# More modulation blocks summed by VectorE, in PSUM; weight splits in quarters, the later ones on GpSimd alone

## The chip, the cores and the metric

One core of a Trainium2 chip runs the whole kernel. The metric is the device time of one execution in microseconds (us), and the median of three such runs of the kernel before is 1456.18 us. The engines are named as the profile names them: PE is TensorE (matmuls), PEld its weight loads, DVE is VectorE, ACT is ScalarE, POOL is GpSimd, SP the engine that issues the loads. Every engine takes its instructions in order.

## What is computed

A layer of a transformer-like encoder on 256 positions of width 2048, all in float32. The parts that matter here, condensed from the reference:

```python
mod = c_act @ w_ada[l] + b_ada[l]
sh1, sc1, g1, sh2, sc2, g2 = [m[:, None, :] for m in jnp.split(mod, 6, axis=-1)]
h = rms_norm(x, g_mix[l]) * (1 + sc1) + sh1
z = h @ w_in                                  # 2048 -> 4616 columns
y = concat([gmlp(u, v), pool(p), attention(q, k, va, fz)]) @ w_out
x = x + g1 * y
h = rms_norm(x, g_ffn[l]) * (1 + sc2) + sh2
x = x + g2 * moe_ffn(h, ...)                  # 16 experts, the router picks 2 for each position
```

The modulation `mod` is one vector (`c_act`, 2048 values) times a matrix of 2048 by 12,288: much weight for little arithmetic. The projections `w_in` and `w_out` are dense products with 256 rows.

## The kernel before

**Split products.** A float32 product is made of three fast ones: each weight tile is split into a high part (a ScalarE cast, L174) and a remainder (one subtraction, L175, on VectorE or GpSimd), written into a buffer `whl`; `mm3` (L177) then issues three matmuls. A weight tile is [128, 4, 512], 1 MB. `halves` (L407) splits it in two halves of [128, 1024] with three buffers of 8 KB for each partition; the first half's remainder is VectorE's, the second half's the engine that `WSPLIT` (for each chunk) or `WSO` (output projection) names. A piece, two halves, has 24 matmuls of 128x512 and needs two PSUM banks `pm`.

**Chunks.** The input projection runs over five chunks of rows of `w_in` (`CHUNKS`, L53): two of 2 row blocks, three of 4. Chunks one and two use `small_piece` (L458), with tiles of two row blocks by 1024 columns: nine blocks of 512 columns, each of 12 matmuls. The others use `piece`, nine pieces each. The first chunk copies its sums into `z` with ScalarE (L436); the others add them with VectorE (L438). The last chunk is woven with the attention (`att_step`, L613, in four parts a to d, for eight heads), gMLP, and pooling. Four pooling bands (`band`, L366) are built in the first chunk by VectorE and GpSimd together. After the chunks comes the output projection (four column blocks of four tiles each), then routing and the experts.

**Modulation blocks.** The modulation's matrix comes in 24 blocks of up to 512 columns, each in steps of 1 MB (four products of 512 columns or eight of 256). A block is done by TensorE in a PSUM bank `accs` (`ada_parts`, L250; a step of four is eight matmul records), or by VectorE as a running sum in SBUF (`sum_parts`, L272, L290 and L292). The strings in L68 say which: `M1A` and `M1B` for shift and scale of the next chunk, `M2A` and `M2B` for the second half of the layer, `G1` for the gate ahead of the output projection. `M1` uses `accs[0]`, `M2` `accs[1]`.

**Order.** The program's order on each engine is written out by hand: `step` (L155) prepares a piece of work (load, split) at once and puts its run (matmuls or sums) into a queue `todo`, which holds up to `LOOK` split pieces and `LOOK_ALL` in all; `PLAN` and `LAST` say after which piece which modulation step comes (`n` and `m`), and when its results are used. Loads go through a ring of six 1 MB halves.

## Time and profile before

| | us |
|---|---|
| median of three runs | 1456.18 (1456.14 to 1457.46) |
| profiled execution | 1460.89 |
| its span in the trace | 1459.1 |
| chunk one, two | 32.37, 41.41 |
| chunk three, four | 67.17, 66.95 |
| last chunk, with attention | 136.99 |
| output projection and the start of the routing | 125.05 |

The lower rows are stretches of the profiled execution. From some 497 us on the routing and the experts run. A row of the timeline begins with its start and its length; in brackets stands the idle time ahead of it on that engine and what ended it. A window's row gives the busy time of PE, PEld, DVE, ACT and POOL in that stretch, then TensorE's granted clock as a share of 2.4 GHz, the DMA share and the rate.

### The profile page before, as it was taken

The numbers are of one execution on the slowest core, as the hardware profiler recorded it, in microseconds if no ns is written. First come the engines' busy times: TensorE is split into PE (matmuls) and PEld (weight loads), VectorE is DVE, ScalarE is ACT, GpSimd is POOL, SyncE is SP. The second block draws the span as 40 slices with busy tenths as digits, with TensorE's granted clock in tenths as the row PEclk, the third lists the DMA queues.
The fourth block names the chain that finished last, engine by engine and source line by source line (L and its number), as shares of the span: only waits on it lengthen the run. The fifth ranks groups of instructions, "written<-read, shape, count | busy, mean of one in ns | idle before, by whom it ended". The sixth has DMA issues, their size and how long they took to land.

```text
span 1459.1 us, 17581 instructions
## 1 busy us (share of the span) xinstructions
PE 1264.6 (87%) x6930; PEld 703.1 (48%) x6930; DVE 693.5 (48%) x1184; ACT 412.8 (28%) x720; POOL 146.0 (10%) x89
## 2 busy tenths in 40 slices
PE   5999999999989997999968999789997879858865
PEld 3666666666667563575324753337633222222221
DVE  3757483555798372795125961169711202202112
ACT  4433333646333240583003840028400000000000
POOL 0423332311333100000000000000000000000000
PEclk8999999999999998999999999999999999979988
DMA  9787787888877868998999989999899999999997
GB/s 378 270 348 281 281 340 265 303 351 328 349 278 270 310 288 367 427 428 317 421 426 427 426 318 419 424 428 426 333 408 428 427 426 427 428 426 428 426 426 303
DMA packets 49207, 539.14 MB, mean 369 GB/s; under 512 B 5464, under 2 KB 5592, under 8 KB 7008
## 3 DMA queue, kind: packets, MB, share of 16 engines
q1 hardware_dynamic: 47664, 534.79, 89.7%
q10 hardware_dynamic: 1456, 3.17, 0.6%
q8 instruction: 56, 0.92, 0.2%
q14 instruction: 31, 0.25, 0.0%
HBM read 535.85 MB, written 2.10 MB: 369 GB/s over the span
## 4 chain that ended last, share of the span: by engine, by line
PE 38%; DMA 27%; DVE 5%; issue 1%; ACT 1%; DVEq 0%; ACTq 0%
PE lbank L170 28%; DMA ring<-in_e_down_dram 11%; DMA ringl<-in_e_gu_dram 9%; DMA ring<-in_e_gu_dram 7%; PE bank L170 5%; PE pm L170 3%; DVE grow L292 2%; PE ada L170 1%; DVE whl L175 1%; DVE el L175 1%; ACT el L174 0%; DVE grow L290 0%; PE lgp L170 0%; DVE hid L1225 0%; PE pt L170 0%
## 5 line engine op out<-in xcount | busy, mean ns | idle before, releaser
L170 PE MATMUL pm<-whl,hT 128*128 128x512 f32 x1120 | 300.9, 405 | 19.9 <-DVE whl L175 10.8
L170 PEld LDWEIGHTS pm<-whl,hT 128*128 128x128 f32 x1120 | 212.3, 193 | 93.6 <-issue 15.3
L170 PE MATMUL lbank<-ringl,xr 128*32 128x256 f32 (+1 forms) x1152 | 143.7, 496 | 38.0 <-DMA ringl<-in_e_gu_dram 37.8
L170 PE MATMUL lbank<-el,xs 128*128 128x512 f32 x576 | 139.9, 401 | 10.2 <-ACT el L174 7.4
L170 PE MATMUL lbank<-ring,xr 128*32 128x256 f32 (+1 forms) x864 | 105.6, 491 | 34.1 <-DMA ring<-in_e_gu_dram 34.0
L174 ACT CAST whl<-ring 128x1024 fp32r<-128x1024 f32 x96 | 99.0, 1048 | 125.7 <-PE pm L170 70.7
L175 POOL TENSOR_TENSOR whl<-ring,whl 128x1024 fp32r<-128x1024 f32 x43 | 108.3, 2518 | 231.7 <-ACT whl L174 211.0
L170 PEld LDWEIGHTS lbank<-el,xs 128*128 128x128 f32 x576 | 109.3, 192 | 41.0 <-ACT el L174 10.6
L170 PE MATMUL bank<-y,gt 128*128 128x512 f32 x240 | 119.1, 619 | 0.0
L1284 DVE TENSOR_TENSOR xa<-xa,bank 128x512 f32<-128x512 f32 x120 | 82.5, 687 | 69.9 <-PE bank L170 69.9
L170 PEld LDWEIGHTS lbank<-ringl,xr 128*32 128x32 f32 (+1 forms) x1152 | 51.9, 128 | 129.8 <-issue 68.5
L170 PE MATMUL lbank<-ring,hidT 128*64 128x512 f32 (+1 forms) x576 | 103.8, 624 | 11.5 <-DMA ring<-in_e_down_dram 11.5
L1275 DVE TENSOR_TENSOR y<-lbank,g2w 128x512 f32<-128x512 f32 x60 | 41.5, 691 | 145.7 <-PE lbank L170 145.7
L174 ACT CAST el<-ring 128x512 fp32r<-128x512 f32 x144 | 89.7, 623 | 29.6 <-PE lbank L170 21.7
L175 DVE TENSOR_TENSOR el<-ring,el 128x512 fp32r<-128x512 f32 x144 | 92.7, 688 | 0.0
L175 DVE TENSOR_TENSOR whl<-ring,whl 128x1024 fp32r<-128x1024 f32 x53 | 72.2, 1368 | 35.9 <-ACT whl L174 33.6
L170 PE MATMUL ada<-ring,cact 128*1 128x512 f32 (+1 forms) x648 | 75.1, 566 | 15.6 <-DMA ring<-in_w_ada_dram 14.4
L1171 ACT COPY gt<-bank 128x256 f32<-128x256 f32 x15 | 5.6, 372 | 287.9 <-PE bank L1169 287.9
L170 PEld LDWEIGHTS lbank<-ring,xr 128*32 128x32 f32 (+1 forms) x864 | 39.5, 128 | 98.4 <-DMA ring<-in_e_gu_dram 48.4
L1225 DVE TENSOR_TENSOR hid<-hid,lbank 128x512 f32<-128x512 f32 x12 | 8.2, 687 | 165.0 <-PE lbank L170 164.7
L170 PE MATMUL lbank<-el,hidT 128*128 128x512 f32 x288 | 74.8, 411 | 12.2 <-DVE el L175 8.3
L438 DVE TENSOR_TENSOR z<-z,pm 128x512 f32<-128x512 f32 x72 | 49.0, 685 | 71.8 <-PE pm L170 71.8
(363 smaller groups left out, 1219.3 us busy)
## 6 DMA issues: line engine op xcount, KB each, us to landing
ringl<-in_e_gu_dram SPq DMA_DIRECT2D x60, 2048.0 KB, 20.1
ring<-in_w_ada_dram SPq DMA_DIRECT2D x90, 1024.0 KB, 7.0
ring<-in_e_gu_dram SPq DMA_DIRECT2D x45, 2048.0 KB, 24.4
ring<-in_e_down_dram SPq DMA_DIRECT2D x45, 2048.0 KB, 25.6
ring<-in_w_in_dram SPq DMA_DIRECT2D x35, 1024.0 KB, 7.0
ringm<-in_e_gu_dram SPq DMA_DIRECT2D x15, 2048.0 KB, 21.7
ringm<-in_e_down_dram SPq DMA_DIRECT2D x15, 2048.0 KB, 21.5
ring<-in_w_out_dram SPq DMA_DIRECT2D x12, 1024.0 KB, 8.3
```

The lines of the kernel that those rows point to most:

```text
L170: E.matmul(out, lhsT=lhsT, rhs=rhs, start=start, stop=stop, skip_group_check=True)
L174: S.copy(hi, src)
L175: (eng or V).tensor_tensor(lo, src, hi.bitcast(F32), op=OP.subtract)
L292: eng.scalar_tensor_tensor(a, w[:, j, :], ck, a, op0=OP.mult, op1=OP.add)
L438: V.tensor_tensor(dst, dst, P[h], op=OP.add)
L1171: S.copy(gt, p[:, :256])
L1225: V.tensor_tensor(hid[:, o], hid[:, o], P[2 * b + 1], op=OP.mult)
L1275: V.tensor_tensor(y, P, g2w[:, c0:c0 + 512], op=OP.mult)
L1284: V.tensor_tensor(a, a, p, op=OP.add)
```

## The change

- **More blocks on VectorE.** `M1A`, `M1B` and `M2A` now name VectorE for all but one of their twelve blocks; nine blocks move, 32 steps. `M2B` stays on TensorE, `G1` as it was.
- **Sums in PSUM.** The running sum lies in the block's PSUM bank `accs`; only the last product writes to SBUF (`ga` or `grow`).
- **Quarters.** `whl` is [128, 2, 512], a quarter of a tile, with six buffers instead of three of twice the size. In chunks one and two the first row block of a tile is split by VectorE and the second by GpSimd; from the third chunk on, and in the output projection, GpSimd makes every remainder. The queue holds four quarters; a modulation step counts as two.
- `PLAN` gives the steps to other pieces; the buffers `hf` are five instead of two; the small matmuls for the forget gate come two places later.

The diff, cut to its core:

```diff
--- before.py
+++ after.py
-LOOK, LOOK_ALL = 2, 2
+LOOK, LOOK_SPLITS = 4, 6
...
 PLAN = [
-    ["n", "n", "n", "n0", "1h"],
-    ["nnn", "n", "0n", "nnn", "1h"],
+    ["nn", "nn", "0", "", "1h"],
+    ["nn", "nn", "nn0", "nn", "1h"],
...
-M1A, M1B, M2A, M2B, G1 = "PPVV", "PPPP", "PPPP", "PPPP", "PVVV"
-WSPLIT, WSO = "VGGGG", "G"
+M1A, M1B, M2A, M2B, G1 = "VVVV", "VPVV", "VVVV", "PPPP", "PVVV"
+WSPLIT, WSO = ["VG", "VG", "GG", "GG", "GG"], "GG"
...
         todo.append((run, prep(), split))
-        while sum(p for _, _, p in todo) > LOOK or sum(x is not None for _, x, _ in todo) > LOOK_ALL:
+        while sum(0 if x is None else 1 if p else 2 for _, x, p in todo) > LOOK:
             run_first()
...
-    def sum_parts(sec, k0, nk, after, eng, tile_of, bias=None):
+    def sum_parts(sec, k0, nk, after, acc, eng, tile_of, bias=None):
         r = 16 // nk
         ng = KD // r
+        P = accs[acc][:, :128 * nk]
...
                     if k == 0:
-                        eng.tensor_scalar(a, w[:, j, :], ck, None, op0=OP.mult)
+                        eng.tensor_scalar(P, w[:, j, :], ck, None, op0=OP.mult)
+                    elif k < KD - 1:
+                        eng.scalar_tensor_tensor(P, w[:, j, :], ck, P, op0=OP.mult, op1=OP.add)
                     else:
-                        eng.scalar_tensor_tensor(a, w[:, j, :], ck, a, op0=OP.mult, op1=OP.add)
+                        a = tile_of()[:, :128 * nk]
+                        eng.scalar_tensor_tensor(a, w[:, j, :], ck, P, op0=OP.mult, op1=OP.add)
...
-    hp, s_hp = pool("hp", LOOK + 1, side="right")
+    hp, s_hp = pool("hp", LOOK_SPLITS, side="right")
...
-        todo.insert(1, (late, None, False)) if todo else late()
+        todo.insert(2, (late, None, False)) if todo else late()
...
-                hl = hp.tile([128, 2, 2, 512], F32R, name="whl")
-                split(hl[:, 0], hl[:, 1], buf[0][:, 2 * a:2 * a + 2, :], engs[a])
+                hl = hp.tile([128, 2, 512], F32R, name="whl")
+                split(hl[:, 0], hl[:, 1], buf[0][:, a, :], engs[a // 2])
                 return hl
...
                 for h in range(2):
-                    for c in range(2):
-                        xh, xl = xs(2 * a + c, h)
-                        mm3(P[h], xh, xl, hl[:, 0, c, :], hl[:, 1, c, :], first and a + c == 0, last and a + c == 2)
-                if a == 1:
+                    mm3(P[h], *xs(a, h), hl[:, 0], hl[:, 1], first and a == 0, last and a == 3)
+                if a == 3:
                     after(P)
             step(prep, run, True)
-        one(0)
-        one(1)
+        for a in range(4):
+            one(a)
...
-    WS = [{"V": V, "G": G}[c] for c in WSPLIT]
+    WS = [[{"V": V, "G": G}[c] for c in x] for x in WSPLIT]
...
-                hl = hp.tile([128, 2, 2, 512], F32R, name="whl")
-                split(hl[:, 0], hl[:, 1], buf[0][:, :, 512 * a:512 * a + 512], (V, WS[q])[a])
+                hl = hp.tile([128, 2, 512], F32R, name="whl")
+                split(hl[:, 0], hl[:, 1], buf[0][:, c, 512 * a:512 * a + 512], WS[q][c])
                 return hl
...
         for a in range(n // 512):
-            one(a)
+            for c in range(2):
+                one(a, c)
...
-        return steps(sum_parts(sec, k0, nk, after_sum, eng, lambda: wk.tile([128, 512], F32, name="ga", bufs=2)))
+        return steps(sum_parts(sec, k0, nk, after_sum, 0 if sec < 2 else 1, eng, lambda: wk.tile([128, 512], F32, name="ga", bufs=2)))
...
-    WO = (V, {"V": V, "G": G}[WSO])
+    WO = [{"V": V, "G": G}[c] for c in WSO]
...
-        return steps(sum_parts(2, 4 * n, 4, lambda a: None, ENG(G1[n]), lambda: r4s[n], n))
+        return steps(sum_parts(2, 4 * n, 4, lambda a: None, n % 2, ENG(G1[n]), lambda: r4s[n], n))
```

In the changed kernel line numbers are one or two off. What the engines' queues hold, at three places:

**GpSimd in the first chunk.** Before, it builds the bands there (`band`; `hf` is the reciprocal that VectorE makes):

```order
L369 IOTA hf 128x256 [waits DVE_49,PE_49]
L373 TENSOR_TENSOR band_134<-hf,tri 128x256 [waits DVE_49]
L374 TENSOR_TENSOR band_134<-band_134,ident 128x128 [waits Pool_49]
L377 TENSOR_TENSOR band_135<-hf,tri 128x128 [waits DVE_49]
L378 TENSOR_TENSOR band_135<-band_135,ident 128x128 [waits Pool_49]
L369 IOTA hf 128x256
L373 TENSOR_TENSOR band_134<-hf,tri 128x256 [waits DVE_49]
```

In the changed kernel, around the first band:

```order
L176 TENSOR_TENSOR whl<-ring_65,whl 128x512 [waits Activation_49]
L370 IOTA hf 128x256
L374 TENSOR_TENSOR band_134<-hf,tri 128x256 [waits DVE_49]
L375 TENSOR_TENSOR band_134<-band_134,ident 128x128 [waits Pool_49]
L378 TENSOR_TENSOR band_135<-hf,tri 128x128 [waits DVE_49]
L379 TENSOR_TENSOR band_135<-band_135,ident 128x128 [waits Pool_49]
L176 TENSOR_TENSOR whl<-ring_63,whl 128x512 [waits DMAHW3_49,Activation_49]
L176 TENSOR_TENSOR whl<-ring_63,whl 128x512 [waits PE_49,Activation_49]
```

Splits now stand ahead of and behind each of the first bands' four products. VectorE's queue there, before and after:

```order
L175 TENSOR_TENSOR whl<-ring_63,whl 128x1024 [waits PE_49,Activation_49]
L370 TENSOR_SCALAR hf<-hf 128x256 [waits Pool_49]
L371 RECIPROCAL hf<-hf 128x256 [waits DVE_49]
L372 SCALAR_TENSOR_TENSOR hf<-jp,hf 128x256 [waits DVE_49]
L376 TENSOR_SCALAR hf<-jp 128x128
L175 TENSOR_TENSOR whl<-ring_64,whl 128x1024 [waits DMAHW4_49,PE_49,Activation_49]
```

```order
L176 TENSOR_TENSOR whl<-ring_63,whl 128x512 [waits DMAHW3_49,Activation_49]
L371 TENSOR_SCALAR hf<-hf 128x256 [waits Pool_49]
L372 RECIPROCAL hf<-hf 128x256 [waits DVE_49]
L373 SCALAR_TENSOR_TENSOR hf<-jp,hf 128x256 [waits DVE_49]
L377 TENSOR_SCALAR hf<-jp 128x128
L288 TENSOR_SCALAR ada_108<-ring_65,cact 128x256 [waits DMAHW1_49]
L290 SCALAR_TENSOR_TENSOR ada_108<-ring_65,cact,ada_108 128x256 [waits DVE_49] x7
L176 TENSOR_TENSOR whl<-ring_63,whl 128x512 [waits PE_49,Activation_49]
```

The split ahead of the band is a quarter, and eight sums of a step follow the band.

**VectorE in the last chunk.** The end of a head's softmax (`s`), the split of a head's result (`ylo`), a scale of the modulation (`mod`), additions to `z`, and the scaling of the next `qk`; before:

```order
L593 TENSOR_SCALAR s<-s,nm 128x256
L175 TENSOR_TENSOR ylo<-pt_114,hT_124 128x256 [waits Activation_49]
L175 TENSOR_TENSOR whl<-ring_63,whl 128x1024 [waits DMAHW2_49,Activation_49]
L324 TENSOR_TENSOR mod<-ada_108,prm_69 128x4 [waits PE_49]
L325 SCALAR_TENSOR_TENSOR mod<-mod,prm_69 128x4 [waits DVE_49]
L438 TENSOR_TENSOR z<-z,pm 128x512 [waits PE_49] x2
L571 TENSOR_SCALAR qk<-pt_115,prm_69 128x256 [waits Activation_49]
```

and in the changed kernel:

```order
L594 TENSOR_SCALAR s<-s,nm 128x256
L176 TENSOR_TENSOR ylo<-pt_114,hT_124 128x256 [waits Activation_49]
L288 TENSOR_SCALAR ada_109<-ring_65,cact 128x512 [waits DMAHW7_49]
L290 SCALAR_TENSOR_TENSOR ada_109<-ring_65,cact,ada_109 128x512 [waits DVE_49] x3
L325 TENSOR_TENSOR mod<-ada_108,prm_69 128x4 [waits PE_49]
L326 SCALAR_TENSOR_TENSOR mod<-mod,prm_69 128x4 [waits DVE_49]
L290 SCALAR_TENSOR_TENSOR ada_109<-ring_65,cact,ada_109 128x512 [waits DMAHW0_49]
L290 SCALAR_TENSOR_TENSOR ada_109<-ring_65,cact,ada_109 128x512 [waits DVE_49] x3
L290 SCALAR_TENSOR_TENSOR ada_109<-ring_63,cact,ada_109 128x512 [waits DMAHW1_49,DVE_49]
L290 SCALAR_TENSOR_TENSOR ada_109<-ring_63,cact,ada_109 128x512 [waits DVE_49] x3
L437 TENSOR_TENSOR z<-z,pm 128x512 [waits PE_49] x2
L572 TENSOR_SCALAR qk<-pt_115,prm_69 128x256 [waits Activation_49]
```

Where one half of a weight tile was split, there are three steps of four sums into `ada_109`, which is `accs[1]`.

**TensorE in the last chunk.** The transposes of a softmax, the product with `va` (`ptr`, `z`), then a step of a modulation block; before:

```order
L600 MATMUL ada_108<-ident,s 128x128 [waits DVE_49]
L600 MATMUL ada_108<-ident,s 128x128 x2
L170 MATMUL pt_115<-ptr,z 128x256 [waits DVE_49]
L170 MATMUL pt_115<-ptr,z 128x128
L170 MATMUL ada_109<-ring_64,cact 1x512 [waits DMAHW3_49]
L170 MATMUL ada_109<-ring_64,cact 1x512 x3
```

and in the changed kernel:

```order
L601 MATMUL ada_108<-ident,s 128x128 [waits DVE_49]
L601 MATMUL ada_108<-ident,s 128x128 x2
L171 MATMUL pt_115<-ptr,z 128x256 [waits DVE_49]
L171 MATMUL pt_115<-ptr,z 128x128
L171 MATMUL ada_109<-ring_64,cact 1x512 [waits DMAHW4_49,DVE_49]
L171 MATMUL ada_109<-ring_64,cact 1x512 x3
L171 MATMUL pt_114<-ones,ga 128x1 x4
```

The product waits for VectorE in both; the modulation step, the first of its block, now waits for VectorE too, whose sums lie in the same bank, and one step of two has gone.

## Rows read from the trace of the kernel before

**Rows 1.** windows of six stages: us, each engine's busy time (instructions), granted clock, DMA share, GB/s

```profile
27.06:59.43 32.37, 31.84 (x176) 22.82 (x177) 22.53 (x24) 19.55 (x29) 9.72 (x15) 0.95 0.84 316
59.43:100.84 41.41, 38.93 (x198) 24.50 (x197) 22.36 (x33) 11.71 (x14) 13.94 (x9) 0.96 0.76 294
100.84:168.01 67.17, 63.31 (x306) 44.82 (x304) 41.81 (x54) 20.57 (x23) 22.49 (x10) 1.00 0.84 336
168.01:234.96 66.95, 63.50 (x306) 44.77 (x305) 43.24 (x54) 21.29 (x24) 22.77 (x10) 1.00 0.77 296
234.96:371.95 136.99, 132.47 (x792) 86.10 (x790) 73.14 (x174) 72.37 (x194) 30.63 (x23) 0.99 0.81 305
371.95:497.00 125.05, 113.93 (x542) 86.56 (x541) 90.46 (x82) 40.91 (x55) 45.38 (x20) 0.95 0.79 302
```

**Rows 2.** timeline, TensorE, third chunk: start, us, operation, count, [idle before <-releaser]

```profile
135.54 5.29 PE L170 MATMUL pm<-whl,hT 128*128 128x512 f32 x22 [1.93 <-DVE whl L175]
...
147.40 1.04 PE L170 MATMUL ada<-ring,cact 128*1 128x512 f32 x8
148.37 5.73 PE L170 MATMUL pm<-whl,hT 128*128 128x512 f32 x24
```

**Rows 3.** groups of VectorE and GpSimd: count | busy us, mean ns | idle before, releasers

```profile
L175 DVE TENSOR_TENSOR whl<-ring,whl 128x1024 fp32r<-128x1024 f32 x43 | 58.5, 1363 | 25.9 <-ACT whl L174 23.6 <-POOL whl L175 2.2
L438 DVE TENSOR_TENSOR z<-z,pm 128x512 f32<-128x512 f32 x72 | 49.0, 685 | 71.8 <-PE pm L170 71.8
...
L292 DVE SCALAR_TENSOR_TENSOR grow<-ringm,cact,grow 128x512 f32<-128x512 f32 x12 | 15.2, 1268 | 0.3
...
L175 POOL TENSOR_TENSOR whl<-ring,whl 128x1024 fp32r<-128x1024 f32 x43 | 108.3, 2518 | 231.7 <-ACT whl L174 211.0 <-DVE z L438 10.6 <-issue 10.2
```

**Rows 4.** chain of waits in the output projection: start, us, what

```profile
422.12 2.79 DVE grow L292
...
424.94 0.76 DVE grow L292
```

**Rows 5.** timeline of VectorE and GpSimd, third chunk

```profile
117.23 0.68 DVE L438 TENSOR_TENSOR z<-z,pm 128x512 f32<-128x512 f32 x1
...
116.58 3.00 POOL L175 TENSOR_TENSOR whl<-ring,whl 128x1024 fp32r<-128x1024 f32 x1 [3.74 <-ACT whl L174]
```

**Rows 6.** timeline, first chunk, around the first band

```profile
38.28 1.75 DVE L371 RECIPROCAL hf<-hf 128x256 f32<-128x256 f32 x1
...
39.70 1.05 ACT L174 CAST whl<-ring 128x1024 fp32r<-128x1024 f32 x1
40.07 0.42 DVE L372 SCALAR_TENSOR_TENSOR hf<-jp,hf 128x256 f32<-128x256 f32 x1
...
40.58 0.74 POOL L373 TENSOR_TENSOR band<-hf,tri 128x256 f32<-128x256 f32 x1 [14.66 <-DVE hf L372]
...
41.39 1.32 POOL L374 TENSOR_TENSOR band<-band,ident 128x128 f32<-128x128 f32 x1
...
43.21 0.46 POOL L378 TENSOR_TENSOR band<-band,ident 128x128 f32<-128x128 f32 x1
```

**Rows 7.** timeline, last chunk, one step of the attention

```profile
300.75 0.92 PE L170 MATMUL pt<-ptr,z 128*128 128x256 f32 x4 [0.33 <-DVE qk L571]
...
301.60 1.04 PE L170 MATMUL ada<-ring,cact 128*1 128x512 f32 x8
...
302.99 0.35 DVE L593 TENSOR_SCALAR s<-s,nm 128x256 f32<-128x256 f32 x1
...
305.50 2.17 DVE L325 SCALAR_TENSOR_TENSOR mod<-mod,prm 128x4 f32<-128x4 f32 x1
...
309.79 0.69 DVE L438 TENSOR_TENSOR z<-z,pm 128x512 f32<-128x512 f32 x1 [2.13 <-PE pm L170]
```

**Rows 8.** timeline, TensorE, output projection, after a wait

```profile
434.87 0.72 PE L170 MATMUL pm<-whl,hT 128*128 128x512 f32 x1 [2.70 <-DVE xg L839]
```

**Rows 9.** window behind that wait, columns as in rows 1

```profile
436.00:438.00 2.00, 2.00 (x7) 1.52 (x6) 0.72 (x1) 1.79 (x5) 0.18 (x1) 0.50 0.99 381
```

More of the change, by code (lines that the diff above doesn't have):

```diff
@@ L367, in band @@
         w = (2, 4, 8, 16)[g]
-        rc = wk.tile([128, T], F32, name="hf")
+        rc = wk.tile([128, T], F32, name="hf", bufs=5)
         G.iota(rc, pattern=[[1, 256]], base=1, channel_multiplier=0, allow_small_or_imprecise_dtypes=True)
@@ L374, in band @@
         G.tensor_tensor(band0[:, g, :128], band0[:, g, :128], ident, op=OP.subtract)
-        rc = wk.tile([128, T], F32, name="hf")
+        rc = wk.tile([128, T], F32, name="hf", bufs=5)
         V.tensor_scalar(rc[:, :128], jp[:, :128], float(w), 1.0 / w, op0=OP.is_lt, op1=OP.mult)
@@ L388, in make_h @@
         hq = hbuf(q)
-        late = None
+        ts = []
         for c in range(nk):
@@ L394, in make_h, with late @@
                 mm(p[:, 128 * h:128 * h + 128], xa[:, h, 128 * k:128 * k + 128], diag[:, h, :])
-            t = wk.tile([128, T], F32, name="hf")
+            t = wk.tile([128, T], F32, name="hf", bufs=5)
             V.tensor_scalar(t, p[:, :T], mod[:, 1, k:k + 1], mod[:, 0, k:k + 1], op0=OP.mult, op1=OP.add)
             split(hq[:, 0, c, :], hq[:, 1, c, :], t)
-            if late is not None:
-                late()
-            def late(k=k, t=t):
+            ts.append((k, t))
+        def late():
+            for k, t in ts:
                 o = 32 * (k % 4)
                 mm(fzp[o:o + 8, :], wfz[:, k, :], t, start=k < 4, stop=k >= KD - 4)
-        todo.insert(1, (late, None, False)) if todo else late()
+        todo.insert(2, (late, None, False)) if todo else late()
     def halves(flat, tile, engs, xs, banks, first, last, after):
@@ L453, in banks, with one @@
             return P
-        halves(win_d, WIN[q, c0], (V, WS[q]), lambda c, h: hpart(q, c, h), banks, True, True,
+        halves(win_d, WIN[q, c0], WS[q], lambda c, h: hpart(q, c, h), banks, True, True,
                lambda P: put(q, c0, P))
     def small_piece(q, c0, n):
-        buf = []
-        def one(a):
+        buf, P = [], []
+        def one(a, c):
             def prep():
-                if a == 0:
+                if a + c == 0:
                     w = ring()[:, :2 * n]
@@ L512, in forget_a @@
     def forget_a():
-        fs = wk.tile([128, 256], F32, name="hf")
+        fs = wk.tile([128, 256], F32, name="hf", bufs=5)
         V.tensor_copy(fs, fzp)
@@ L659, in pool_mix @@
                 mm(p[:, 128:256], z[:, 1, c0:c0 + 128], band1[:, g, :], start=False)
-                d = wk.tile([128, 256], F32, name="hf")
+                d = wk.tile([128, 256], F32, name="hf", bufs=5)
                 V.tensor_copy(d, p[:, :256])
```

15 lines of the change are left out of this document (6 added, 9 removed).

## The prediction

> **What bounds the kernel now.** I read the busy time stage by stage first [rows 1]. The six rows are the four earlier chunks of the input projection, the last chunk (with attention, gMLP and pooling), and the output projection with what leads to the routing. TensorE is busy 98%, 94%, 94%, 95%, 97% and 91% of them: all are TensorE's, and the last holds the most idle time, 125.05 - 113.93 = 11.1 us. The experts that follow take their loads' pace and start only after the routing; their instructions are untouched, so the change is worth what it takes from these 470 us.
>
> Next, TensorE's timeline in the third chunk [rows 2]. A piece of 24 matmuls takes 5.73 us, and the step of 8 ahead of it runs from 147.40 to 148.37: 0.97. The gain offered is therefore about 0.97 us for each modulation step that leaves TensorE, and there are 32: by stage 4, 4, 6, 6, 12 and none.
>
> Then the price elsewhere [rows 3]. A half's split takes 1.36 us on VectorE and 2.52 on GpSimd in the mean. A VectorE sum in SBUF takes up to 1.27 in the mean (those from ringm), while the addition to z, which reads PSUM, has one length, 0.685, seventy-two times.
>
> The chain through the output projection says why the sums are long there [rows 4]: a sum of 2.79 and the next of 0.76 follow each other there with a gap of 0.03. This stage waits for VectorE.
>
> **Sums in PSUM.** Beside a GpSimd split that took 3.00 us, the addition from PSUM still ran 0.68 [rows 5]. I take a PSUM sum at the undisturbed pitch of the sum in SBUF, 0.76 and a gap [rows 4], 3.1 us for a step of four; bounds 2.7 (four at the 0.685 of the addition) and 5.1 (four at 1.27) [rows 3]. The Trainium skill (SBUF — State Buffer, Who interferes with whom) says that a VectorE instruction with at most one SBUF input, outside its two-port modes, doesn't contend with GpSimd, and one with two SBUF inputs does; the 0.68 and the 2.79 agree, and by it the lower bound is the nearer one.
>
> **Splits by GpSimd alone.** The trace has no split of 512; half of 2.52 is 1.26, with 0.06 between instructions 1.32, so 5.3 us a piece against TensorE's 5.7 [rows 2, 3]. It fits by 0.4 us, and six buffers let it run a piece ahead. If the old contention stayed, a quarter would be half of 3.00 and more, 1.5 to 1.6.
>
> **Chunk three and four** (67.17 and 66.95 us, [rows 1]). Six steps each leave TensorE: 6 x 0.97 = 5.8. Idle time of 3.9 in the third (67.17 - 63.31) is mostly the wait for VectorE's splits, such as the 1.93 at 135.54 [rows 2]: gone. New: where two sum steps, 6.2 us, lie between two additions to z, a piece of 5.7 can't hide them, and its PSUM banks come back late: +1.7. Sum **-8.0** each (bounds -10 and -1).
>
> **Output projection** (125.05). VectorE loses its 16 half splits and keeps 12 sum steps of 3.1, in a column block four, 12.4; GpSimd has 16 quarters of 1.32, 21; TensorE's busy time is 113.93 / 4 = 28.5. So TensorE paces, and its 11.1 us of idle time [rows 1] goes except for about 1 at the start. After it had stood 2.70 us its granted clock from 436 to 438 was 0.50, 1.2 GHz [rows 8, 9]: two us for what takes one at 2.4 GHz. Two such waits go, 1.2 each. Sum **-12.5** (bounds -14 and -6).
>
> **First chunk** (32.37). Here the order hurts. GpSimd now splits the second quarter of each pair, and three of the four bands' products stand ahead of a split that this chunk needs, while the products wait for VectorE's reciprocal, itself queued behind VectorE's own quarter. From that quarter on it is 1.75 + 0.42 on VectorE, 0.74 + 1.32 and two of 0.46 on GpSimd [rows 6], then 1.26: 6.4 us, of which TensorE covers 6 matmuls, 1.4. That is 5.0 a band, 15.0 for three. Before, VectorE split everything here, and no split stood behind the products. ScalarE's copies of z now stand ahead of the next tile's casts in two tiles: a cast of half of 1.05 each [rows 6], 1.0 together. Against this, four steps of 0.97 go (-3.9), and with them what is now idle or slow, 32.4 - 25.8 - 3.9 = 2.7 (nine blocks of half a piece, 2.87, and the steps). That gives +9.4; since the eight-wide sums on VectorE come on top and splits run a block ahead by the third band, I take **+10** (bounds +2, if two of the bands are overtaken by earlier work, and +20, if the sums, two runs of eight a tile, come wholly on top).
>
> **Second chunk** (41.41). Four steps go, -3.9; VectorE gets splits, four additions and two sum steps in a pair of blocks, some 10 us against 5.7: **+1**.
>
> **Last chunk** (136.99). Twelve steps leave TensorE: -11.6. The sums now stand in VectorE's queue between the attention's parts. Three places pay:
> - The next modulation block stays on TensorE and begins in the same PSUM bank, so its first matmul waits for the last sum. In the trace TensorE starts such a step at 301.60, while VectorE's softmax runs to 303.34; with 3.1 behind it the bank is free at 306.4: 4.8 late [rows 7]. Three blocks end so, one beside other matmuls: 12.
> - Twice three sum steps, 9.3 us, lie between a head's split of y and the additions to z. Today VectorE has 6.4 us there, from 303.34 to 309.79, with a small operation of 2.17 and a split in them [rows 7]; TensorE's next product needs the bank that the qk scaling behind those additions reads. About 4 each: 8.
> - Three single steps in place of a split of 1.36 are 1.7 longer each; about half of it shows: 3.
> Together 23 - 11.6, less 2 for waits of today that fall into the new ones: **+9** (bounds -6, if half of the 12 is all that shows, and +22, if each of the twelve steps shows in full, 37 - 11.6 - 3).
>
> **Clock.** The new waits of about five us are longer than the 2.70 that ended in 0.50 [rows 8, 9]; part of the slow stretch lies where others are late anyhow: **+2** (0 to +6).
>
> **Sum.** +10 + 1 - 8 - 8 + 9 - 12.5 + 2 = **-6.5 us**. The profiled execution took 1460.89, so 1454.4; it was 4.71 above the median of the timed runs, 1456.18, so the median becomes **1449.7**.
>
> **The rivals.**
> - *TensorE paces everything.* The loads of the sums arrive early, VectorE works ahead, and the waits of the first and the last chunk mostly vanish: +2 and -6 in place of +10 and +9, no clock loss: -6.5 - 8 - 15 - 2 = -31.5, **1424.7**. For it: VectorE was busy 73 of 137 us in the last chunk [rows 1]. Against it: its queue is in order, and the three places above need no overload.
> - *VectorE's queue decides* (slower). Every sum step of the last chunk shows in full, +22, and the first chunk pays +18: -6.5 + 13 + 8 = +14.5, **1470.7**. It turns the sign as soon as the two chunks together lose 26 us instead of 19. For it: the 0.33 at 300.75 shows that a product already waits for the qk scaling [rows 7]. Against it: not all sums stand next to a softmax.
> - *GpSimd becomes the pace* (slower). If its quarter takes 1.6, as the 3.00 beside VectorE would have it [rows 5], a piece takes 6.4 to 6.6 against 5.7: 9 x 0.9 = 8 lost in each of chunks three and four and half of that in the last chunk; the output projection's columns have room for 16 x 1.6 = 26. -6.5 + 20 = +13.5, **1469.7**. Against it: the additions from PSUM that nothing stretched.
> - *The loads cap it*, so that it doesn't do what it says. The stages move 294 to 336 GB/s at DMA shares of 0.76 to 0.84 [rows 1]; a stage an eighth shorter wants above 0.9, and six ring halves held longer by sums may not give it. Half the gain of chunks three and four and a third of the last stage's goes: -6.5 + 12 = +5.5, **1461.7**.
>
> **How the numbers follow.** The forecast has 0.40, the first rival 0.15, VectorE's queue 0.24, GpSimd 0.11, the loads 0.10. What a measurement of this kernel can tell from no change is about 0.2%, 2.9 us. The forecast's own spread (1440 to 1460) gives 0.31 faster, 0.05 the same, 0.04 slower; the first rival is all faster; the slower ones with their milder forms give 0.04 faster, 0.09 the same, 0.32 slower. So faster 0.50, same 0.14, slower 0.36. The range goes from between the first rival and the forecast, 1428, to just above the slower ones, 1474.
>
> **What would show it.** In the new profile: chunks three and four at 59 us with GpSimd splits at 1.26 and TensorE never waiting for them; the output projection near 112 us with TensorE busy throughout; first chunk near 42 us, with TensorE waiting for a GpSimd split after each of the first bands; last chunk near 146, with waits of a modulation matmul for VectorE's sum and of a product for qk. PSUM sums much above 0.78, or GpSimd quarters above 1.4, would overturn the middle terms; no waits in the first chunk, the largest loss.

## The result, and the profile after

The changed kernel is slower. Its median is 1472.34 us (1468.74 to 1475.77) against 1456.80 for the kernel before in the same measurement: a ratio of 1.0106, 95% interval 1.0081 to 1.0132. The forecast was 1449.7, a gain; 1472.34 lies just inside the range's upper end, but on the other side of no change. The profiled execution took 1471.45 us, with a span of 1469.7.

The same stages as in [rows 1], windows of the changed kernel (us, then busy time of PE, PEld, DVE, ACT and POOL with their instructions, TensorE's granted clock, DMA share, GB/s). The last row ends with the output projection's last matmul, which in the kernel before lies at 496.09:

```profile
25.22:68.70 43.48, 31.98 (x113) 23.57 (x114) 33.20 (x56) 20.74 (x38) 20.62 (x25) 0.84 0.67 260
68.70:121.51 52.81, 40.65 (x165) 26.82 (x164) 32.55 (x51) 12.21 (x23) 16.78 (x17) 0.84 0.65 238
121.51:185.03 63.52, 58.97 (x257) 47.39 (x256) 46.52 (x70) 22.07 (x40) 46.89 (x38) 0.92 0.84 321
185.03:243.13 58.10, 54.77 (x257) 44.09 (x256) 45.36 (x70) 21.78 (x40) 44.04 (x36) 1.00 0.85 336
243.13:399.14 156.01, 133.63 (x695) 91.66 (x694) 96.82 (x210) 72.46 (x209) 52.52 (x48) 0.89 0.76 279
...
399.14:504.94 105.80, 105.55 (x534) 82.77 (x533) 50.97 (x70) 44.79 (x85) 84.24 (x67) 1.00 0.91 356
```

The reader is to see three columns. The lengths: the first, second and last stages grew by 11.1, 11.4 and 19.0 us, the others shrank. TensorE's busy time: in the last chunk 133.63, where it was 132.47, although twelve modulation steps (11.6 us) have left it. And the clock: 0.84, 0.84, 0.92 and 0.89, where [rows 1] have 0.95, 0.96, 1.00 and 0.99. The busy time that the steps gave back was taken again by matmuls at the lower clock.

The two prices on which the middle of the prediction stood, from the groups of the changed kernel (count | busy us, mean ns | idle before, releasers):

```profile
L290 DVE SCALAR_TENSOR_TENSOR ada<-ring,cact,ada 128x512 f32<-128x512 f32 x159 | 120.0, 755 | 4.7
```

```profile
L176 POOL TENSOR_TENSOR whl<-ring,whl 128x512 fp32r<-128x512 f32 x174 | 221.8, 1306 | 166.4 <-ACT whl L175 161.3 <-issue 4.0 <-POOL prm L622 1.0
```

A PSUM sum took 0.755 us and a GpSimd quarter 1.306: forecast were 0.76 and 1.26 (1.32 with the gap).

**First two chunks.** TensorE's timeline of the changed kernel (start, us, operation, count, [idle before <-releaser]):

```profile
39.09 6.35 PE L171 MATMUL pm<-whl,hT 128*128 128x512 f32 x16 [4.29 <-POOL whl L176]
...
53.31 6.07 PE L171 MATMUL pm<-whl,hT 128*128 128x512 f32 x16 [4.29 <-POOL whl L176]
...
72.42 1.23 PE L171 MATMUL pt<-diag,xa 128*128 128x128 f32 x4 [2.67 <-DVE mod L325]
...
91.37 4.39 PE L171 MATMUL pm<-whl,hT 128*128 128x512 f32 x11 [3.12 <-DVE z L437]
...
103.64 4.21 PE L171 MATMUL pm<-whl,hT 128*128 128x512 f32 x9 [3.13 <-DVE z L437]
```

In the first chunk TensorE waits for a GpSimd split that stands behind a band's products. In the second it waits first for the chunk's `mod`, which VectorE makes behind its part of the fourth band (69.62 to 72.16), and then for additions to `z`, which must read a PSUM bank before it is free. VectorE's timeline there shows what the additions stand behind:

```profile
82.08 1.37 DVE L437 TENSOR_TENSOR z<-z,pm 128x512 f32<-128x512 f32 x2 [2.10 <-PE pm L171]
83.36 0.69 DVE L176 TENSOR_TENSOR whl<-ring,whl 128x512 fp32r<-128x512 f32 x1
83.97 0.75 DVE L288 TENSOR_SCALAR ada<-ring,cact 128x512 f32<-128x512 f32 x1
84.75 2.34 DVE L290 SCALAR_TENSOR_TENSOR ada<-ring,cact,ada 128x512 f32<-128x512 f32 x3
87.00 0.69 DVE L176 TENSOR_TENSOR whl<-ring,whl 128x512 fp32r<-128x512 f32 x1
87.60 3.12 DVE L290 SCALAR_TENSOR_TENSOR ada<-ring,cact,ada 128x512 f32<-128x512 f32 x4
90.63 1.27 DVE L437 TENSOR_TENSOR z<-z,pm 128x512 f32<-128x512 f32 x2
```

Eight sums, 6.2 us, and two quarters lie between two pairs of additions; [rows 2] give a piece 5.73.

**Last chunk.** VectorE, then TensorE:

```profile
314.30 0.74 DVE L288 TENSOR_SCALAR ada<-ring,cact 128x512 f32<-128x512 f32 x1
315.08 2.34 DVE L290 SCALAR_TENSOR_TENSOR ada<-ring,cact,ada 128x512 f32<-128x512 f32 x3
...
318.19 6.29 DVE L290 SCALAR_TENSOR_TENSOR ada<-ring,cact,ada 128x512 f32<-128x512 f32 x8
324.38 1.28 DVE L437 TENSOR_TENSOR z<-z,pm 128x512 f32<-128x512 f32 x2
...
328.95 2.33 DVE L290 SCALAR_TENSOR_TENSOR ada<-ring,cact,ada 128x512 f32<-128x512 f32 x3
331.31 0.75 DVE L293 SCALAR_TENSOR_TENSOR ga<-ring,cact,ada 128x512 f32<-128x512 f32 x1
```

```profile
282.21 0.76 PE L568 MATMUL pt<-ident,z 128*128 128x128 f32 x5 [1.24 <-DVE z L557]
286.84 0.80 PE L171 MATMUL ada<-qk 128*128 128x128 f32 x2 [3.86 <-DVE qk L572]
...
314.48 8.97 PE L171 MATMUL pm<-whl,hT 128*128 128x512 f32 x24 [1.30 <-ACT whl L175]
...
332.12 1.89 PE L171 MATMUL ada<-ring,cact 128*1 128x512 f32 x8 [5.08 <-DVE ga L293]
...
341.46 1.04 PE L171 MATMUL ada<-ring,cact 128*1 128x512 f32 x8
...
372.02 0.95 PE L601 MATMUL pt<-ident,s 128*128 128x128 f32 x3 [3.45 <-DVE s L593]
...
375.64 1.89 PE L171 MATMUL ada<-ring,cact 128*1 128x512 f32 x8 [1.39 <-DVE ga L293]
```

The step at 332.12 starts the next block in the bank whose last sum, at 331.31, VectorE has just finished: the wait that was foreseen at [rows 7], 5.08 instead of 4.8. But the step then takes 1.89 instead of 1.04, and a piece of 24 matmuls at 314.48 takes 8.97 instead of 5.73 (both in [rows 2]). Windows of the changed kernel behind a wait of the first chunk, inside that piece, and behind the wait of 5.08:

```profile
39.10:45.40 6.30, 6.30 (x16) 4.68 (x16) 5.50 (x11) 1.76 (x3) 1.47 (x2) 0.59 0.69 235
316.00:320.00 4.00, 4.00 (x10) 3.13 (x11) 3.86 (x7) 0.00 (x0) 3.49 (x3) 0.50 0.55 182
332.10:341.10 9.00, 8.98 (x36) 6.74 (x37) 1.90 (x6) 0.83 (x3) 0.76 (x1) 0.50 0.64 233
```

After 5.08 us idle TensorE was granted 0.50, that is 1.2 GHz, for nine us in which it was never idle.

### The profile page after: what moved, and what is told of

The parts are those of the page before. It is cut to its first block, busy times and chain, and to the rows that moved or that the text cites. A ratio compares the mean times of both kernels' runs of the same rounds, so it can differ in the third digit from the quotient of the medians.

```text
span 1469.7 us, 17439 instructions
## 1 busy us (share of the span) xinstructions
PE 1250.6 (85%) x6642; PEld 709.3 (48%) x6642; DVE 706.6 (48%) x1289; ACT 420.0 (29%) x815; POOL 266.9 (18%) x232
## 4 chain that ended last, share of the span: by engine, by line
PE 57%; DMA 27%; DVE 9%; issue 3%; ACT 2%; POOL 2%; SPq 0%; DVEq 0%; POOLq 0%; ACTq 0%
PE lbank L171 29%; PE pm L171 16%; DMA ring<-in_e_down_dram 11%; DMA ringl<-in_e_gu_dram 7%; DMA ring<-in_e_gu_dram 7%; PE bank L171 6%; PE ada L171 3%; DVE ada L290 3%; PE pt L171 2%; POOL whl L176 1%; DMA ring<-in_w_ada_dram 1%; DMA ring<-in_w_in_dram 1%; DVE z L437 1%; DVE el L176 1%; PE lgp L171 1%
## 5 line engine op out<-in xcount | busy, mean ns | idle before, releaser
L171 PE MATMUL pm<-whl,hT 128*128 128x512 f32 x1120 | 310.4, 416 | 31.7 <-POOL whl L176 11.4
L171 PEld LDWEIGHTS pm<-whl,hT 128*128 128x128 f32 x1120 | 219.8, 200 | 96.1 <-POOL whl L176 16.5
L176 POOL TENSOR_TENSOR whl<-ring,whl 128x512 fp32r<-128x512 f32 x174 | 221.8, 1306 | 166.4 <-ACT whl L175 161.3
L171 PE MATMUL lbank<-el,xs 128*128 128x512 f32 x576 | 136.8, 395 | 8.2 <-ACT el L175 5.2
L175 ACT CAST whl<-ring 128x512 fp32r<-128x512 f32 x192 | 108.8, 618 | 113.4 <-DMA ring<-in_w_in_dram 72.7
L171 PE MATMUL lbank<-ring,xr 128*32 128x256 f32 (+1 forms) x864 | 108.7, 508 | 33.7 <-DMA ring<-in_e_gu_dram 33.7
L290 DVE SCALAR_TENSOR_TENSOR ada<-ring,cact,ada 128x512 f32<-128x512 f32 (+1 forms) x187 | 133.7, 715 | 5.6
L175 ACT CAST el<-ringl 128x512 fp32r<-128x512 f32 x96 | 58.3, 622 | 77.4 <-DMA ringl<-in_e_gu_dram 64.3
```

The source lines that it names most:

```text
L171: E.matmul(out, lhsT=lhsT, rhs=rhs, start=start, stop=stop, skip_group_check=True)
L175: S.copy(hi, src)
L176: (eng or V).tensor_tensor(lo, src, hi.bitcast(F32), op=OP.subtract)
L290: eng.scalar_tensor_tensor(P, w[:, j, :], ck, P, op0=OP.mult, op1=OP.add)
```

## Experiments

The theory from the traces: the blocks cost the first, second and last chunks, by sums ahead of what TensorE waits for and by the clock behind each wait; the quarters, the PSUM sums and the splits by GpSimd are a gain by themselves. Against it stood that GpSimd's splits set the pace, that the loads did, or that quarters made the waits. All ratios are to the kernel before, run beside each. The medians of that kernel in these measurements lie between 1456.80 and 1460.43, so a difference of 3 or 4 us between two experiments says little by itself.

**1. The last chunk's blocks back on TensorE** (the changed kernel with one string changed; this also puts two steps back into each of chunks three and four).

```diff
-M1A, M1B, M2A, M2B, G1 = "VVVV", "VPVV", "VVVV", "PPPP", "PVVV"
+M1A, M1B, M2A, M2B, G1 = "VVVV", "VPVV", "PPPP", "PPPP", "PVVV"
```

> The changed kernel with the four M2A blocks back on TensorE (16 steps of sums leave VectorE: 2 each in chunks three and four, 12 in the last). Theory A (VectorE's queue between the parts of the attention, and the slow clock after the waits, cost the last chunk its 19 us): the last chunk falls from 156.0 to about 137 to 140, its granted clock from 0.89 to 0.98 or more, chunks three and four gain 2 us each, the median falls by 12 to 16 us, to about 1458. Theory B (the quarters and GpSimd's splits cost it): the last chunk stays above 150, since 12 steps of 0.97 come back to TensorE, and the median rises or stays at 1472. Theory C (ring halves held by the sums delay loads): like A in time, but the waits that go are ScalarE's for loads.

Measured 1453.30, ratio 0.9957 (0.9934 to 0.9979): 19 us under the changed kernel, more than expected. Its last chunk:

```profile
241.74:380.94 139.20, 132.45 (x791) 85.51 (x790) 61.48 (x162) 73.92 (x212) 53.40 (x48) 0.99 0.85 312
```

Busy again 132.45, at a clock of 0.99, idle 6.8 where the changed kernel has 22.4. The twelve steps, worth 11.6 us, cost 28 in this stage. Chunks three and four, with two steps more each on TensorE, took 61.6 and 57.9, not longer than 63.5 and 58.1: there the last two steps taken off TensorE had brought nothing.

**2. The bands ahead of everything.** Where in the changed kernel the four bands come between the first pieces, they are built here before the first norm.

```diff
+    for i in range(4):
+        band(i)
+
     ssx = cst.tile([128, 2], F32, name="ssx")
...
-            if q == 0 and i < 4:
-                then(lambda i=i: band(i))
```

> The changed kernel with the four pooling bands built ahead of the first loads' use, where VectorE and GpSimd stand idle, and not between the splits of the first chunk. Theory A (GpSimd's quarter behind a band's products): the two waits of 4.29 us for GpSimd go, with the slow clock behind them, the first chunk falls from 43.5 to about 33 to 35 and the median by 8 to 10 us. Theory B (quarters and casts behind the copies of z): the waits for GpSimd shrink, the first chunk stays above 39 because VectorE's runs of eight sums or ScalarE's casts are next, and the median falls by less than 4 us.

Measured 1468.96, ratio 1.0067 (1.0043 to 1.0091). First chunk, and the row of TensorE's timeline ahead of it:

```profile
33.72:68.17 34.45, 27.44 (x112) 20.21 (x113) 24.17 (x44) 20.73 (x38) 14.47 (x11) 1.00 0.64 236
```

```profile
25.89 1.46 PE L171 MATMUL ada<-ring,cact 128*1 128x256 f32 x12 [10.46 <-ACT r L307]
```

The stage lost 9.0 us and all its waits for GpSimd, and its clock is 1.00; but it began at 33.72 instead of 25.22, since the norm's chain stood behind the bands on VectorE. So the cause is right and the place only moved the cost. The median fell by 3.4 where 8 to 10 were expected. In the trace that is not a rest of the 9.0, which the later start (8.5) takes back: the second chunk took 47.72 instead of 52.81, with the wait for `mod` behind the fourth band gone, and the last chunk 158.07, 2.1 more.

**3. The second chunk's sums back on TensorE.**

```diff
-M1A, M1B, M2A, M2B, G1 = "VVVV", "VPVV", "VVVV", "PPPP", "PVVV"
+M1A, M1B, M2A, M2B, G1 = "VPVV", "VPVV", "VVVV", "PPPP", "PVVV"
```

> The changed kernel with one block, the shift that is summed during the second chunk, back on TensorE (4 steps). Theory A (sums ahead of the additions to z on VectorE, and through them ring halves that come free late, make the second chunk's 52.8 us): the second chunk falls to about 42 to 44, TensorE's two waits of 3.1 us for the additions go, ScalarE's waits for loads (2.5 and 10.8 us) shrink below 3, and the median falls by 8 to 10 us. Theory B (splits in quarters are what the second chunk waits for): it stays above 49 and the median falls by less than 3 us.

Measured 1458.29, ratio 0.9989 (0.9969 to 1.0009), 14 us under the changed kernel, more than expected.

```profile
70.62:112.81 42.19, 39.03 (x197) 25.50 (x196) 22.88 (x35) 12.82 (x24) 16.54 (x17) 0.92 0.78 295
```

The chunk takes 42.19 instead of 52.81 although TensorE has four steps more. So 10.6 of the 11.4 us lost there hang on these four sum steps.

**4. The old blocks with everything else new**: `PLAN` and the block strings as before, first chunk split by VectorE alone, and quarters, PSUM sums and GpSimd splits from the third chunk on.

```diff
...
-M1A, M1B, M2A, M2B, G1 = "VVVV", "VPVV", "VVVV", "PPPP", "PVVV"
-WSPLIT, WSO = ["VG", "VG", "GG", "GG", "GG"], "GG"
+M1A, M1B, M2A, M2B, G1 = "PPVV", "PPPP", "PPPP", "PPPP", "PVVV"
+WSPLIT, WSO = ["VV", "VG", "GG", "GG", "GG"], "GG"
```

> Quarters, six buffers, sums in PSUM and GpSimd's splits from chunk three on and in the output projection as in the change, but the blocks, the plan and the first chunk's splits (VectorE alone) as before. Theory A (only the moved blocks and the first chunk's split cost): first, second and last chunk near 32, 41 and 136 us, the output projection 18 us shorter than before to the last matmul, the median about 1456 - 20 = 1436. Theory B (quarters and GpSimd's splits cost as such): first, second and last chunk 3 to 8 us longer than before each, and the median above 1448.

Measured 1437.76, ratio 0.9851 (0.9820 to 0.9882): faster than before by 1.5%. The output projection, from its first to its last matmul, took 105.79 us (before 124.14):

```profile
367.86:473.65 105.79, 105.54 (x534) 82.76 (x533) 50.20 (x70) 44.71 (x85) 84.23 (x67) 1.00 0.92 356
```

Two stages grew. The last chunk took 140.8 instead of 136.99, with 3.1 us of waits for ScalarE's casts and GpSimd's quarters that the kernel before doesn't have. The third took 70.5 instead of 67.17; TensorE's timeline there:

```profile
129.10 1.89 PE L171 MATMUL ada<-ring,cact 128*1 128x512 f32 x8 [3.81 <-DVE ga L293]
```

It is the wait of the last chunk again: a block on TensorE starts in the bank in which VectorE has just been summing.

**5. The blocks of chunks three and four on VectorE too**, on top of experiment 4.

```diff
-M1A, M1B, M2A, M2B, G1 = "PPVV", "PPPP", "PPPP", "PPPP", "PVVV"
+M1A, M1B, M2A, M2B, G1 = "PPVV", "PPVV", "PPPP", "PPPP", "PVVV"
```

> The kernel with the old blocks and plan, quarters and GpSimd's splits (1437.8), and of the change's moved blocks only the two scale blocks that are summed during chunks three and four (8 steps leave TensorE). Theory A (a moved block pays where VectorE has nothing else in its queue but additions to z, and where the other block in the same PSUM bank doesn't have to wait for its sum): chunk three falls from 70.5 to about 60, its wait of 3.8 us for the last sum goes, chunk four from 61.6 to about 57.5, the median by 13 to 15 us to about 1423. Theory B (moved blocks cost wherever they are, through GpSimd or the loads): the two chunks together fall by less than 6 us.

Measured **1424.56** (1423.52 to 1426.37), ratio 0.9752 (0.9713 to 0.9790): the fastest of all kernels here, 33 us under the kernel before. Windows of the third, the fourth and the last chunk:

```profile
95.49:157.08 61.59, 59.02 (x273) 45.35 (x272) 40.65 (x62) 21.77 (x40) 46.43 (x38) 0.97 0.86 347
157.08:215.02 57.94, 56.78 (x273) 44.21 (x272) 39.69 (x62) 22.67 (x41) 44.27 (x36) 1.00 0.87 335
215.02:354.27 139.25, 131.19 (x792) 84.28 (x790) 61.48 (x162) 73.97 (x212) 53.37 (x48) 1.00 0.84 312
```

Here the move pays: four steps off TensorE in each of chunks three and four, no PSUM bank in which the two engines take turns, and a clock of 0.97 to 1.00. The first two chunks took 30.24 (from the first matmul) and 39.00. So two of the nine moved blocks were worth 13 us; the other seven, with the order and the shared split of the first chunk that come with them, cost 48 (1472.34 - 1424.56).

**6. Experiment 4 with the splits shared as before** (VectorE one row block, GpSimd the other).

```diff
-WSPLIT, WSO = ["VV", "VG", "GG", "GG", "GG"], "GG"
+WSPLIT, WSO = ["VV", "VG", "VG", "VG", "VG"], "VG"
```

> Old blocks and plan, sums in PSUM and quarters, but the splits shared by VectorE and GpSimd as before (two quarters of a tile each, VectorE alone in the first chunk). Theory A (the output projection's gain of 18 us needs VectorE free of its splits): about half of it goes, the output projection is 7 to 12 us longer than the 103.9 with GpSimd alone, the median 1444 to 1450. Theory B (the gain is that of sums in PSUM, which GpSimd doesn't stretch): the output projection stays within 3 us of 103.9 and the median within 4 us of 1437.8.

Measured 1443.15, ratio 0.9874 (0.9831 to 0.9917), 5.4 us over experiment 4, with intervals that overlap. Output projection:

```profile
371.30:478.90 107.60, 106.51 (x534) 82.47 (x533) 76.59 (x97) 44.48 (x85) 47.87 (x35) 1.00 0.90 351
```

The 103.9 of the expectation is a window that began 1.84 us after the first matmul; from the first to the last it is 105.79. So GpSimd alone is worth 1.8 us there (107.60 to 105.79), within Theory B's 3; the median is between the two theories. More of the 5.4 lies in chunks three and four (73.95 and 63.90 here, 70.53 and 61.60 in experiment 4).

**7. Experiment 4 with the sums in SBUF**, as before.

```diff
-        P = accs[acc][:, :128 * nk]
...
+                if g == 0:
+                    buf.append(tile_of()[:, :128 * nk])
...
-                        eng.scalar_tensor_tensor(P, w[:, j, :], ck, P, op0=OP.mult, op1=OP.add)
+                        eng.scalar_tensor_tensor(a, w[:, j, :], ck, a, op0=OP.mult, op1=OP.add)
```

> Old blocks and plan, quarters, GpSimd's splits from chunk three on, but the VectorE sums in SBUF as in the kernel before. Theory A (GpSimd's splits and sums with two inputs in SBUF hold each other up, so PSUM is needed once GpSimd splits everything): VectorE's sums are 1.2 us or more in the mean, GpSimd's quarters 1.5 or more, the output projection 8 us or more longer than 103.9, the median 1446 to 1455. Theory B (where the sums lie doesn't matter): the output projection within 3 us of 103.9, sums at 0.76; and chunk three is some 5 us shorter, because TensorE's next block doesn't wait for a PSUM bank.

Measured 1457.80, ratio 0.9983 (0.9962 to 1.0004): the gain of experiment 4 is gone, and the median is above Theory A's 1455. Output projection, the largest group of VectorE's sums into `grow`, all of them in that stage, and the splits of GpSimd:

```profile
370.20:491.70 121.50, 114.80 (x533) 84.03 (x532) 90.42 (x70) 44.52 (x85) 103.98 (x67) 0.96 0.83 310
```

```profile
L293 DVE SCALAR_TENSOR_TENSOR grow<-ring,cact,grow 128x512 f32<-128x512 f32 x33 | 50.9, 1541 | 1.1
```

```profile
L176 POOL TENSOR_TENSOR whl<-ring,whl 128x512 fp32r<-128x512 f32 x165 | 233.4, 1447 | 121.5 <-ACT whl L175 116.4 <-issue 4.0 <-POOL prm L622 0.9
```

A sum takes 1.54 us instead of 0.755, and GpSimd's quarter 1.447 instead of 1.297 in experiment 4. Together this closes a table of the output projection, from its first to its last matmul:

| us | splits shared | GpSimd alone |
|---|---|---|
| sums in SBUF | 124.14 (before; half splits) | 121.50 (7) |
| sums in PSUM | 107.60 (6) | 105.79 (4) |

The sums' place is worth 15.7 by the right column (the upper left cell also has the old halves and queue), the splits' engine 1.8 by the lower row. The Trainium skill (SBUF — State Buffer, Who interferes with whom) has the rule that a VectorE instruction with two SBUF inputs contends with a GpSimd instruction that reads SBUF, and one with at most one, outside the two-port modes, does not; 1.54 against 0.755 beside the same GpSimd work agrees.

**8. The waits filled.** The changed kernel, with constant matmuls whose results nothing uses issued ahead of four waits (two in the first chunk, two in the last).

```diff
...
+                if sec == 4 and g == 0 and k0 == 8:
+                    for _ in range(FILL):
+                        mm(lgfill, ident, tri)
...
```

> The changed kernel with matmuls of constants (8 to 10 of 128x256, about 0.41 us each, results unused) on TensorE in four of its long waits: two for GpSimd in the first chunk, one for a sum's bank and one for a softmax in the last. No wait is taken away. Theory A (the slow granted clock that follows the waits, not only the waits, makes the loss): the granted clock behind these places stays at 1.0, the first chunk falls by 4 to 5 us, the last by 8 to 9, the median by 10 to 14 although work is added. Theory B (the clock falls for another reason, or the time behind the waits is hidden): the clock behind the places is 0.5 as before, or the median stays within 3 us of 1472.

Measured 1464.77 (ratio 1.0037, 1.0015 to 1.0060), 7.6 us under the changed kernel, with more work. Its profiled execution is the fastest of its ten, 5 us under their median, so its stages flatter it somewhat. TensorE's timeline and a window behind a filled wait:

```profile
34.31 4.48 PE L172 MATMUL ada<-tri,ident 128*128 128x256 f32 x20
38.77 4.37 PE L172 MATMUL pm<-whl,hT 128*128 128x512 f32 x16
...
329.53 1.04 PE L172 MATMUL ada<-ring,cact 128*1 128x512 f32 x8 [0.77 <-DVE ga L298]
...
334.49 1.04 PE L172 MATMUL ada<-ring,cact 128*1 128x512 f32 x8
```

```profile
329.50:338.50 9.00, 8.97 (x58) 6.47 (x59) 2.95 (x10) 2.61 (x8) 2.08 (x2) 1.00 0.83 297
```

The 16 matmuls, at 39.09 in the changed kernel, start at 38.77 and take 4.37 instead of 6.35; the step takes 1.04 instead of 1.89, and the window behind it has a clock of 1.00 instead of 0.50. The waits stay, only filled. So the clock behind a wait is a cost of its own, and four waits of many carried some 8 us of it. That is Theory A's cause with less than its size: the last chunk fell by 7.4 (148.58), the first by 2.1 only (41.37), since a wait of 1.20 for VectorE's split took part of it back, and 10 to 14 were expected in all.

**9. The second chunk's splits to GpSimd**: does VectorE wait there because of its two quarters?

```diff
-WSPLIT, WSO = ["VG", "VG", "GG", "GG", "GG"], "GG"
+WSPLIT, WSO = ["VG", "GG", "GG", "GG", "GG"], "GG"
```

> The changed kernel with the second chunk's splits on GpSimd alone: VectorE keeps its sums and its additions to z there, and loses two quarter splits in each pair of blocks. Theory A (the two sum steps, 6.2 us ahead of the additions to z, are what the second chunk waits for): its two waits of 3.1 us shrink by the splits' 1.4 at most, the chunk stays at 47 to 51 and the median falls by 2 to 5 us. Theory B (VectorE's splits behind the sums are what it waits for): the chunk falls to 43 to 45, the median by 8 or more. Theory C (only loads that come late): the chunk stays at 52 to 53.

Measured 1470.02, ratio 1.0064 (1.0036 to 1.0092); the chunk took 53.5 us, no less than 52.8.

```profile
93.00 7.10 PE L171 MATMUL pm<-whl,hT 128*128 128x512 f32 x24 [4.17 <-DVE z L437]
...
104.25 4.21 PE L171 MATMUL pm<-whl,hT 128*128 128x512 f32 x9 [4.15 <-DVE z L437]
```

The chunk's length is Theory C's, and Theory A's 47 to 51 missed; but 2.0 us of it are a longer wait for `mod` behind the fourth band (4.67 instead of 2.67). The waits for `z` are 4.2 instead of 3.1: without the splits the additions still stand behind the sums. So it is the sums and not the splits. No run tells apart how much of the 11.4 comes from ring halves that late sums hold (here, too, the casts then wait 11.2 us for a load). The trace of the changed kernel speaks for the queue: VectorE works without a gap from 82.08 to 91.90 and from 95.04 to 104.19, so the additions that end the two waits of 3.1 come late by what stands ahead of them there, and not by a load.

**10. Experiment 5 with the first chunk's split shared**, and no sums in that chunk.

```diff
-WSPLIT, WSO = ["VV", "VG", "GG", "GG", "GG"], "GG"
+WSPLIT, WSO = ["VG", "VG", "GG", "GG", "GG"], "GG"
```

> The kernel with the old blocks, the two scale blocks of chunks three and four on VectorE and GpSimd's later splits (1424.6), with one thing of the change more: the first chunk's second quarters split by GpSimd, behind the bands' products. No sums stand in the first chunk. Theory A (the order on GpSimd, band products ahead of a split, costs the first chunk its time): two or three waits of 4 to 5 us for GpSimd appear, with a slow clock behind them, the first chunk grows from 32.2 to 41 to 45 and the median to 1433 to 1438. Theory B (it was the eight-wide sums on VectorE): the first chunk grows by less than 4 us.

Measured 1433.83, ratio 0.9817 (0.9781 to 0.9853) against experiment 5's 0.9752. The first chunk took 39.9 us instead of 30.2, a little less than the 41 expected, at a clock of 0.91. TensorE's timeline has this wait twice, and one of 0.58, where two or three of 4 to 5 us were expected:

```profile
39.52 1.20 PE L171 MATMUL pm<-whl,hT 128*128 128x512 f32 x4 [2.58 <-POOL whl L176]
```

GpSimd's order, bands ahead of a split, costs 9.7 us of this chunk without a single sum. The changed kernel's first chunk is 3.6 longer, although TensorE has four steps less there; how much of that is the sums and how much the other plan was not tested.

## Why the prediction was wrong

Stage by stage, with the change split into the steps that left TensorE (0.97 each, [rows 2]), its idle time (stage less busy time, both tables of windows) and what is left of its busy time, mostly the clock:

| us | forecast | measured | steps gone | idle | rest of busy |
|---|---|---|---|---|---|
| ahead of the first chunk | 0 | -1.8 | | | |
| first chunk | +10 | +11.1 | -3.9 | +11.0 | +4.0 |
| second chunk | +1 | +11.4 | -3.9 | +9.7 | +5.6 |
| third chunk | -8 | -3.7 | -5.8 | +0.7 | +1.5 |
| fourth chunk | -8 | -8.9 | -5.8 | -0.1 | -2.9 |
| last chunk | +9 | +19.0 | -11.6 | +17.9 | +12.8 |
| output projection | -12.5 | -18.3 | 0 | -10.9 | -7.5 |
| from there to the experts' first load | 0 | +2.3 | | | |
| clock | +2 | (in the rows) | | | |

Sum +11.1 (the span grew by 10.6) where -6.5 was forecast; 17.6 us are to be explained. The medians differ by more, 22.6, because the prediction carried over that the profiled execution of before lay 4.71 above its median; the changed kernel's lay 0.89 below. Nothing was changed ahead of the first chunk: its first matmul came at 24.6 to 27.1 in the runs, experiment 2 aside. And the fourth row shows that the last column is not the clock alone: at 1.00 before and after, 2.9 went, of which 1.8 are the eight small matmuls for the forget gate (2.4 us before, 0.6 now).

**The clock: the term that failed most.** It was +2, with +6 as its end. In the first three chunks and the last the busy time beyond the steps rose by 4.0 + 5.6 + 1.5 + 12.8 = 24 us, while the granted clock fell from 0.95 to 1.00 before to 0.84 to 0.92. The prediction saw the effect at one place [rows 8, 9], priced it as 1.2 us for a wait, and then argued that the slow stretch "lies where others are late anyhow". It doesn't: behind the wait at 332.12 TensorE worked nine us without a gap at 0.50, and up to the step at 341.46 that took 9.34 us, where the same matmuls took 4.96 in experiment 8 (329.53 to 334.49). So that one wait of 5.08 cost 4.4 more. Experiment 8 shows the clock as a cause: the same waits, filled, and 7.6 us go. For the remaining waits the 24 us are the traces' sum, not an experiment's; the third chunk's 1.5 holds the same gain as the fourth's, so its clock cost more than it shows.

**The second chunk: a missed mechanism.** The step "some 10 us against 5.7: +1" saw that VectorE was overloaded and then booked almost nothing for it. By its own figures two pairs of blocks with sums are 2 x 4.3 = 8.6 over, less 3.9: +4.7. In the third chunk the same pattern was given its rule, that sums between two additions hold the PSUM banks; it wasn't carried to the second. Experiment 3 puts 10.6 of the 11.4 on the four sum steps, and experiment 9 rules out VectorE's splits. The causes overlap: without touching the sums, experiment 2 takes 5.1 off this chunk by moving the bands. Of TensorE's 12.2 us of idle time here, 6.3 end with an addition to `z`, 2.8 with a quarter of VectorE, 2.7 with `mod` behind the fourth band, and 0.5 with ScalarE.

**The last chunk: the waits smaller than forecast, and the clock on top.** Forecast were 23 us of new waits less 2; the idle time rose by 17.9. The bank that passes from VectorE's sum to TensorE's next block cost 5.08 at one block, 1.39 at another and nothing at the third: 6.5 where 12 were forecast. The two runs of three sum steps cost 0.37 (326.11; the slow piece at 314.48 covers the rest) and 3.45, for a softmax and not for `qk`: 3.8 where 8 were forecast. The single steps cost 1.24 and 3.86, 5.1 instead of 3; that the 3.86 is near the "about 4" of another place is chance. Waits for ScalarE's casts, 3.6, were not named. The error of +10 in this row is the 12.8 of busy time, less 3 of waits that didn't come. Experiment 1 shows the whole: without these twelve steps the stage takes 139.2, still 2.2 more than before; experiments 4 and 5, which have the quarters too, took 140.8 and 139.25 there.

**The first chunk: the right cause, and the right size by luck.** +11.1 against +10, with GpSimd's split behind the bands as the cause (4.29, twice). Experiment 2 takes these waits out of the stage (-9.0), experiment 10 gives 9.7 us for the order on GpSimd alone. But the working, 5.0 for each of three bands and 1.0 for casts less the gains, didn't hold: the third band's wait was 0.52, and the idle time rose by 11.0. What made up for it is the clock: the prediction took 2.7 of idle and slow time off, and the busy time beyond the steps rose by 4.0 at 0.84.

**Chunks three and four.** -3.7 and -8.9 against -8 each. The fourth is right in size, with the small matmuls' gain in it, and has the one wait for `z` (1.33). In the third, half the gain went, and not by late PSUM banks, the term that the prediction had there: no wait for `z` shows. The clock was 0.92, and TensorE's longest wait ended with a cast of ScalarE that had waited for a load:

```profile
153.07 0.84 PE L171 MATMUL pm<-whl,hT 128*128 128x512 f32 x2 [2.41 <-ACT whl L175]
...
152.40 2.18 ACT L175 CAST whl<-ring 128x512 fp32r<-128x512 f32 x4 [7.14 <-DMA ring<-in_w_in_dram]
```

That load was issued at 144.00, behind one at 143.57, which had waited for the ring half of a sum step that ended at 143.54. Experiment 5, where two of the six steps stay on TensorE in each of these chunks, got -5.6 and -9.0 from 67.17 and 66.95.

**The output projection: right, and too small.** TensorE hardly waits (idle 0.25), its clock went from 0.95 to 1.00, and its busy time fell from 113.02 to 105.55, where 2.4 were forecast for two waits. Of the two reasons that the prediction gave, the price of a PSUM sum, taken from [rows 4, 5], decided it (15.7, experiment 7); that VectorE loses its splits is worth 1.8 (experiment 6). The Trainium skill (GPSIMD Engine Reference, 3.1 Elementwise) measures GpSimd at 1.96 times VectorE's time for the same addition of 2048 columns; here a quarter took 1306 ns against 688 for VectorE's split of that size in the experts, 1.90 times. That the slower engine is no worse here, and in one profiled execution of each kernel 1.8 us better, is experiment 6.

**The rivals.** "VectorE's queue decides" gave 1470.7 and a chance of 0.24; the measured 1472.3 is nearest to it, and the traces show its mechanism, sums ahead of what TensorE waits for. The number is in part luck: it had +18 for the first chunk (11.1), nothing for the second, where the same mechanism cost 11.4, and no more for the clock. "TensorE paces everything" is refuted by the waits. GpSimd's pace is refuted by 1.306. That the transfer rate caps the stages is refuted by DMA shares of 0.65, 0.67 and 0.76 in the very stages that grew; the other half of that rival, ring halves held longer by sums, does show, in the third chunk.
